# Block sums stored in one transfer each, and new places in the order for FFN weights, sum reads and three x tiles

## The chip, the cores and the metric

The kernel runs on one core of one Trainium2 chip. The metric is device time in microseconds (us), the median of several runs. A core has five engines that run side by side, each through its own instructions in order: TensorE (PE, matmuls; its weight loads are listed as PEld), VectorE (DVE), ScalarE (ACT), GpSimd (POOL) and SyncE (SP), which here issues all transfers to and from DRAM.

## The reference

One step of a hybrid layer over 128 context tokens and 1024 latent tokens of width 1024, in float32:

```
h  = rmsnorm(x) * (1 + scale1) + shift1
u  = h @ w_in                       # pool part, LRU part, gate part
mix = concat(pool_mixer(u_pool), rg_lru(conv(u_x)) * gelu(u_gate)) @ w_out
x  = x + gate1 * rmsnorm(mix)
h2 = rmsnorm(x) * (1 + scale2) + shift2
gu = h2 @ w_ffn_in                  # d_ff = 2816
x  = x + gate2 * rmsnorm((silu(gu[:d_ff]) * gu[d_ff:]) @ w_ffn_out)
```

The scales, shifts and gates come from a conditioning vector through a modulation matrix; the LRU is a gated linear scan in both directions.

## The kernel before, in words

The 1152 tokens are nine tiles of 128 rows (tile 0 is the context), in three groups of 384 columns once transposed. Each float32 operand is split into a rounded part and a rest (names with h or HT, and l or LO); a product is three matmuls, h*h, h*l and l*h. The helper `split` writes the rounded part by a copy (L315 on ACT, L317 on DVE, whichever the planner picks) and the rest by a subtraction on DVE (L346).

The code doesn't issue instructions directly. It lists operations, and a planner (class `Sched`) runs a model of the engines and takes again and again the operation that can start first; among equals the lower priority number wins, which is the place in the program plus `S.shift`. What it decides is each engine's order; on the chip each engine keeps to it and waits where something isn't there yet. Buffers come from small pools: three "raw" buffers of 512 KB, four "f", six "ring" and so on, and five banks "ps", two "pt", one "pm" for matmul results.

Stages that matter here:

- `stage_x(t)` loads an x tile, computes its root mean square (L309, L366 to L369), scales it (L456 or L458), transposes it by eight matmuls with the identity (L466, four to a bank) and copies the banks into stage buffers (L481, L483). `make_h` modulates these (L524, L526) and splits them into HT and LO. `gemm_in` (L533) multiplies them with w_in. Tiles 6 to 8 are the last column group; their gemm is 72 matmuls for the first three units of weights (`M0`).
- `mod_group` multiplies the second modulation matrix (L862: 16 matmuls in the order, 32 records in the trace).
- `post_mix(t)`, in the order of tiles 0, 4, 1, 5, 2, 6, 3, 7, 8, takes a tile's output gemm, multiplies it with the gate rows (L333, `s<-ps,grow`), norms it, adds it to x (L995), stores it (`x1d`), scales it (L456 or L458, `s<-xt,r`), transposes it (L466) and makes `hf`, HT and LO of the FFN.
- `combos(t)` for tiles 4 to 7 builds four sums of blocks of a pair of tiles, splits each into a raw buffer `tp` and stores it to the DRAM tensor `tdr` (L963).
- `FW(f)` loads one FFN weight block (two transfers of 512 KB, `rw<-in_w_fi`, into raw buffers) and `split` makes `wq` of it. `load_T` and `load_T1` read the sums back (`T`, and the right half of HT and LO). The FFN's first block is plain matmuls (L533 with `wq`), the later ones use the sums (L1235).

`combos` and `FW` share the raw pool; all transfers share SP's queue.

Of the kernel before, what the change touches and what calls it, by code (L numbers as in the profile page):

```python
# [7 lines left out]
F32 = mybir.dt.float32  # L8
# [34 lines left out]
TABLE_PEN = 400  # L43
DMA_AHEAD = 1.0
TABLE_WAIT = 1.0
TSH = (0, 60, 60)
STEPS = "p1 p8 p6 p2 tr8 p7 cx p5 xpz p4 p3 hi_gate hi_out store"
LASTK = 2
ORDER = "L0 F0 L1 F1 L2 P3 L3 P2 P1 P0 F2 F3"
# [2 lines left out]
KREV = (7,)  # L52
KG = 4
MODG = (1, 2, 2, 4)
LATE_STEP = 40
XPS = (1, 2)
SHIFTS = (-150, -100)
# [221 lines left out]
def kernel(ctx: ExitStack, tc: tile.TileContext, x, cT, vec, rows, w_modA, w_modB, w_in, w_gate,  # L279
                      w_pool, w_out, w_fi, w_fo, y, st_out):  # L280
    nc = tc.nc
# [3 lines left out]
    dram = ctx.enter_context(tc.tile_pool(name="dram", bufs=1, space=bass.MemoryType.DRAM))  # L285
# [3 lines left out]
    S = Sched(counts)  # L289

    def sb(name, tag="s", shape=(128, T), dt=F32, n=1):
        return S.buf(tag, lambda: sp.tile(list(shape), dt, name=name, tag=tag, bufs=counts[tag]), n)

    def bank(tag="ps"):
        return S.buf(tag, lambda: psp.tile([128, 512], F32, name=tag, tag=tag, bufs=counts[tag]))
# [39 lines left out]
    def dma(dst, src, w, r, nbytes, q="SP"):  # L335
        return S.op((("SP", nbytes / DMA_RATE),), lambda e: nc.sync.dma_start(dst(), src()), r, w)
# [7 lines left out]
    def split(src, h, l, w_h, w_l, r, n):  # L344
        anycopy(h, src, w_h, r, n)
        dve(lambda: nc.vector.tensor_tensor(l(), src(), h().bitcast(F32), op=OP.subtract), w_l, list(r) + list(w_h), n)  # L346

    class Unit:
        def __init__(self, src, tag="ring"):
            raw = sb("raw", "raw", (128, 1024))  # L350
            dma(lambda: raw.t, lambda: src, raw.all(), [], 524288)
            self.h = h = sb("uh", tag, (128, 1024), F32R)
            self.l = l = sb("ul", tag, (128, 1024), F32R)
            split(lambda: raw.t, lambda: h.t, lambda: l.t, h.all(), l.all(), raw.all(), 1024)
# [47 lines left out]
    def K(name, ks, ts):  # L402
        return (HT if name == "H" else LO).k(ks, ts)

    def TT(tg):
        return range(3 * tg, 3 * tg + 3)
# [65 lines left out]
    def stage_x(t):  # L472
        S.tag = f"x{t}"
        xt = xs.pop(t)

        def consume(g, pt):
            def fn(e):
                for i in range(4):
                    d, p = stage[4 * g + i].t[:, t * 128:(t + 1) * 128], pt.t[:, i * 128:(i + 1) * 128]
                    if e == "ACT":  # L480
                        nc.scalar.activation(d, p, AF.Copy)  # L481
                    else:
                        nc.vector.tensor_copy(d, p)  # L483
            S.op((("ACT", 0.65), ("DVE", 0.8)), fn, pt.all(), [stage[4 * g + i][t] for i in range(4)])
        norm_T(xt, consume, None, ("ps", "ps") if t in XPS else ("pt", "pt"))

    def mod_quarter(q, ws):
        S.tag = f"modq{q}"
        pm = bank("pt")
        g = MODG[q]  # L490
        for i in range(0, 4, g):
# [24 lines left out]
    def make_h(k, tg):  # L516
        S.tag = f"h{k}{tg}"
        parts = [(0, 128, 0), (128, 384, 1)] if tg == 0 else [(tg * TG, (tg + 1) * TG, 1)]
        sk = [stage[k][t] for t in TT(tg)]
        for a, b, v in parts:  # L520
            def mod(e, a=a, b=b, v=v):
                d, sc, bi = stage[k].t[:, a:b], s1[:, k, v:v + 1], b1[:, k, v:v + 1]
                if e == "ACT":
                    nc.scalar.activation(d, d, AF.Identity, bias=bi, scale=sc)  # L524
                else:
                    nc.vector.tensor_scalar(d, d, sc, bi, op0=OP.mult, op1=OP.add)  # L526
            S.op(c_act(b - a, ptr=2) + c_dve(b - a, True, 2), mod, [("mod1", k // 2)], sk)
        c = slice(tg * TG, (tg + 1) * TG)
        split(lambda: stage[k].t[:, c], lambda: HT[:, k, c], lambda: LO[:, k, c], K("H", [k], TT(tg)),
              K("L", [k], TT(tg)), sk, TG)  # L530
# [38 lines left out]
    def evac(m, tg, p):  # L569
        if m < 4:  # L570
            evac_x(m, tg, p)
        else:
            if m not in mix:
                mix[m] = sb(f"mix{m}", n=3)
            g = mix[m]
            anycopy(lambda: g.t[:, tg * TG:(tg + 1) * TG], lambda: p.t[:, :TG], [g[tg]], p.all(), TG, True)
# [4 lines left out]
    for a in START.split():  # L581
        i = int(a[1:])
# [30 lines left out]
    for m in M0:  # L613
        for tg in range(2):
            evac(m, tg, pend[m][tg])
    for t in range(6, 9):
        stage_x(t)
    for k in range(KT):
        make_h(k, 2)
    for m in M0:  # L620
        pend[m][2] = bank()
        gemm_in(wu[m], pend[m], range(KT), (2,))
        evac(m, 2, pend[m][2])
# [286 lines left out]
    for n, a in enumerate(ORDER.split()):  # L910
        j = int(a[1:])
# [34 lines left out]
    hfs = {}  # L946
    HN = 512
    PAIR = (4, 5, 6, 7)
    tdr = dram.tile([4, 4, 128, 2, HN], F32, name="tdr")

    def combos(t):

        S.tag = f"T{t}"
        a, b = hfs.pop(t - 4), hfs.pop(t)
        c = slice(t * 128, (t + 1) * 128)
        ca = slice((t - 4) * 128, (t - 3) * 128)
        b11, b21, b12, b22 = ((lambda h=h, i=i: h.t[:, 4 * i:4 * i + 4]) for h, i in ((a, 0), (a, 1), (b, 0), (b, 1)))
        k11, k21, k12, k22 = ([h[k] for k in range(4 * i, 4 * i + 4)] for h, i in ((a, 0), (a, 1), (b, 0), (b, 1)))
        def put(i, e):
            o = sb(f"tp{i}", "raw", (128, 2, 4, 128), F32R, n=2)  # L960
            split(lambda: e.t, lambda: o.t[:, 0], lambda: o.t[:, 1], [o[0]], [o[1]], e.all(), 512)
            for kt in range(4):
                S.op((("SP", 0.6),), lambda _, kt=kt: nc.sync.dma_start(  # L963
                    tdr[i - 1, kt, :, :, ca], o.t[:, :, kt].bitcast(F32)), o.all(), [("td", i, kt, t)])
        d = sb("d", "gw", (128, 4, 128))
        tt(lambda: d.t, b12, b11, d.all(), k12 + k11, 512, OP.subtract)
        put(1, d)
        e = sb("e", "gw", (128, 4, 128))
        tt(lambda: e.t, b22, b12, e.all(), k22 + k12, 512, OP.subtract)
        put(3, e)  # L970
        tt(lambda: e.t, lambda: e.t, b11, e.all(), k11, 512, OP.add)
        put(2, e)
        tt(lambda: e.t, b21, lambda: e.t, e.all(), k21, 512, OP.subtract)
        put(4, e)
# [46 lines left out]
    FORD = [f for i in range(HF) for f in (i, HF + i)]  # L1021

    class FW:

        def __init__(self, f):
            self.raw, self.q = [], []
            for i in range(2):
                raw = sb("rw", "raw", (128, 1024))  # L1030
                dma(lambda raw=raw, i=i: raw.t, lambda i=i: w_fi[f, i], raw.all(), [], 524288)
                self.raw.append(raw)

# [35 lines left out]
    for t in TORD:  # L1069
        if t not in pg:  # L1070
            gout(t)
        if t in TORD[:2]:
            continue
        for u in TORD[:3] if t == TORD[2] else (t,):
            post_mix(u, pg[u])
            if u in PAIR[:-1]:
                combos(u)
            if u == PAIR[-2]:
                fw0 = FW(FORD[0])
                fw0.split(0)  # L1080
                fw0.split(1)
    combos(PAIR[-1])
# [61 lines left out]
    def load_T(i):  # L1144
        S.tag = f"Tl{i}"
        for kt in range(4):
            o = TT_[i, kt] = sb(f"T{i}", "s", (128, 2, HN), F32R)
            dma(lambda o=o: o.t.bitcast(F32), lambda i=i, kt=kt: tdr[i - 1, kt], o.all(),
                [("td", i, kt, t) for t in PAIR], 524288)

    def load_T1():
        S.tag = "Tl1"
        c = slice(HN, 2 * HN)
        for kt in range(4):
            for j, (X, n) in enumerate(((HT, "H"), (LO, "L"))):
                dma(lambda kt=kt, X=X: X[:, kt, c].bitcast(F32), lambda kt=kt, j=j: tdr[0, kt, :, j], K(n, [kt], PAIR),
                    [("td", 1, kt, t) for t in PAIR], 262144)

    def operand(i, kt):
        if i in (1, "B11", "B21", "B22"):  # L1160
# [156 lines left out]
    load_T(2)  # L1317
    S.shift = TSH[0]
    load_T(3)
    S.shift = TSH[1]  # L1320
    load_T1()
    S.shift = TSH[2]
    load_T(4)
# [196 lines left out]
    p = product("E1", gsl(0, H1), gk(0), "11", t8)  # L1520
# [10 lines left out]
    p = product("E5", ssl(0), lambda kt: [("s12", kt)], "11", t8, ("11", "12", "11"))  # L1531
# [4 lines left out]
    p = product("E6", ssl(1), lambda kt: [("s12", kt)], "11", None, ("11", "22", "11"))  # L1536
# [4 lines left out]
    p = product("E7", gsl(0, H2), gk(0), "12", None, ("12", "22", "12"))  # L1541
# [4 lines left out]
    p = product("E4", gsl(HF, H2), gk(HF), "11", None, ("11", "11", "21"))  # L1546
# [7 lines left out]
    p = product("E2", gsl(HF, H1), gk(HF), "21", t8)  # L1554
# [8 lines left out]
    p = product("E3", ssl(2), lambda kt: [("s4", kt)], "22", t8, None, TAIL)  # L1563
# [3 lines left out]
    for n, (i, h) in enumerate(late):  # L1567
        S.shift = -LATE_STEP * n
        add(h[1], h[1], p[i])
# [89 lines left out]
```

## Time and profile before

| what | value |
|---|---|
| median of three runs | 1091.43 us (1089.12 to 1091.92) |
| profiled execution, its own time | 1093.47 us |
| its span in the trace | 1091.7 us |
| PE busy | 1070.3 us, 98% of the span |
| VectorE busy | 782.5 us, 72% |
| ScalarE busy | 491.2 us, 45% |
| the chain that ended last | 91% PE, 4% DVE, 2% DMA |

The span is the time from the first to the last recorded instruction of one execution; the run's own time lies 1.8 us above it. A busy share is a mean over stages: whether an engine ends a wait is read in the stage. The granted clock is PE's, 1.00 for 2.4 GHz and 0.50 for 1.2 GHz.

### The profile page before, as it was taken

What the parts mean: (1) busy time and instruction counts of PE and PEld (TensorE: products, weight loads), DVE (VectorE), ACT (ScalarE), POOL (GpSimd) and SP (SyncE); (2) the same over time, 40 slices, a digit from 0 to 9 for tenths busy, and PEclk for the clock granted to TensorE, in tenths of its full rate; (3) what the DMA queues carried; (4) which work ended last, traced back from release to release, by engine and by line L of the source; (5) the groups of instructions that cost most, each with busy time, mean ns of one, the idle gap of its engine ahead of it and who ended that gap; (6) DMA issues with size and microseconds to landing.
All of it is one profiled execution on the core that took longest, in us unless ns stands there. A gap on an engine that the chain in (4) does not pass through costs nothing.

```text
span 1091.7 us, 14516 instructions
## 1 busy us (share of the span) xinstructions
PE 1070.3 (98%) x5505; PEld 912.4 (84%) x5505; DVE 782.5 (72%) x1428; ACT 491.2 (45%) x891; POOL 8.8 (1%) x54
## 2 busy tenths in 40 slices
PE   7999999999999899999999999999999999999997
PEld 6988899998888888888888888888888888888885
DVE  5756899994987657658467575584667978878876
ACT  7656888872866423234233232332324223233331
POOL 0010000000000000000000000000000000000000
PEclk9989999999999899999999999999999999999999
DMA  9835631132555872314223233141246953353612
GB/s 364 314 120 210 217 117 44 59 133 99 181 186 155 283 287 82 111 39 150 82 68 113 86 102 111 39 150 73 78 154 223 379 174 105 88 175 107 217 53 97
DMA packets 68664, 158.88 MB, mean 146 GB/s; under 512 B 6241, under 2 KB 26097, under 8 KB 68593
## 3 DMA queue, kind: packets, MB, share of 16 engines
q1 hardware_dynamic: 68592, 157.95, 41.8%
q8 instruction: 43, 0.70, 0.3%
q14 instruction: 29, 0.23, 0.1%
HBM read 118.45 MB, written 39.47 MB: 145 GB/s over the span
## 4 chain that ended last, share of the span: by engine, by line
PE 91%; DVE 4%; DMA 2%; ACT 1%; issue 0%; SPq 0%; DVEq 0%; ACTq 0%
PE ps L533 33%; PE ps L1235 32%; PE pm L533 10%; PE pt L533 8%; PE pt L1235 5%; DMA raw<-in_w_in 2%; PE pm L862 1%; PE pt L466 1%; DVE e L333 1%; ACT jk L309 1%; DVE x L1496 1%; PE pt L496 1%; DMA rw<-in_w_fi 0%; DVE tp L346 0%; DVE s L333 0%
## 5 line engine op out<-in xcount | busy, mean ns | idle before, releaser
L533 PE MATMUL ps<-bw,au 128*128 128x512 f32 x627 | 164.4, 391 | 0.0
L533 PEld LDWEIGHTS ps<-bw,au 128*128 128x128 f32 x627 | 117.7, 188 | 25.8
L1235 PE MATMUL ps<-T,wu 128*128 128x512 f32 x504 | 123.1, 393 | 0.2
L1235 PE MATMUL ps<-HT,wu 128*128 128x512 f32 x336 | 111.4, 392 | 0.0
L1235 PEld LDWEIGHTS ps<-T,wu 128*128 128x128 f32 x504 | 92.8, 188 | 21.2 <-ACT wq L315 1.0
L315 ACT ACTIVATE au<-araw 128x512 fp32r<-128x512 f32 x73 | 46.0, 631 | 135.5 <-PE ps L533 88.6
L533 PE MATMUL ps<-HT,uh 128*128 128x384 f32 x280 | 84.9, 345 | 4.3 <-ACT HT L315 2.2
L533 PE MATMUL ps<-HT,ul 128*128 128x384 f32 x280 | 83.8, 341 | 1.3 <-DVE a L362 1.3
L533 PE MATMUL ps<-LO,uh 128*128 128x384 f32 x280 | 83.9, 341 | 0.1
L1235 PEld LDWEIGHTS ps<-HT,wu 128*128 128x128 f32 x336 | 63.1, 188 | 13.8
L1235 PE MATMUL ps<-LO,wu 128*128 128x512 f32 x168 | 65.5, 390 | 0.0
L309 ACT ACTIVATE g<-g 128x512 f32<-128x512 f32 x42 | 26.6, 632 | 83.7 <-DVE g L333 83.4
L315 ACT ACTIVATE wq<-rw 128x512 fp32r<-128x512 f32 x66 | 40.3, 628 | 52.7 <-DMA rw<-in_w_fi 46.2
L1235 PE MATMUL ps<-T,wq 128*128 128x512 f32 x252 | 61.0, 390 | 0.0
L533 PE MATMUL pm<-wq,HT 128*128 128x512 f32 x168 | 60.4, 397 | 0.0
L346 DVE TENSOR_TENSOR wq<-rw,wq 128x512 fp32r<-128x512 f32 x88 | 58.1, 684 | 2.9 <-ACT wq L315 2.7
L315 ACT ACTIVATE wu<-q 128x512 fp32r<-128x512 f32 x64 | 40.1, 632 | 42.1 <-DVE q L333 42.1
L333 DVE TENSOR_TENSOR wu<-q,wu 128x512 fp32r<-128x512 f32 x84 | 56.8, 686 | 1.8 <-ACT wu L315 1.4
L533 PEld LDWEIGHTS ps<-HT,uh 128*128 128x128 f32 x280 | 52.4, 192 | 6.6 <-issue 3.6
L1235 PE MATMUL ps<-HT,wq 128*128 128x512 f32 x168 | 56.6, 389 | 0.0
L1235 PE MATMUL pt<-HT,wq 128*128 128x512 f32 x168 | 55.7, 393 | 0.0
L533 PE MATMUL pt<-bw,au 128*128 128x512 f32 x198 | 55.1, 390 | 0.0
(314 smaller groups left out, 2211.5 us busy)
## 6 DMA issues: line engine op xcount, KB each, us to landing
rw<-in_w_fi SPq DMA_DIRECT2D x44, 512.0 KB
mraw<-in_w_modB SPq DMA_DIRECT2D x32, 512.0 KB
gdr<-g SPq DMA_DIRECT2D x21, 576.0 KB
araw<-gdr SPq DMA_DIRECT2D x20, 512.0 KB
xt<-in_x SPq DMA_DIRECT2D x18, 512.0 KB
wm<-in_w_modA SPq DMA_DIRECT2D x16, 512.0 KB
tdr<-tp SPq DMA_DIRECT2D x64, 128.0 KB
rows<-in_w_fo SPq DMA_DIRECT2D x16, 512.0 KB
```

The costliest lines, as they stand in the source:

```text
L309: nc.scalar.activation(dst(), src(), func, **k)
L315: nc.scalar.activation(dst(), src(), AF.Copy)
L333: return dve(lambda: nc.vector.tensor_tensor(dst(), a(), b(), op=op), w, r, n)
L346: dve(lambda: nc.vector.tensor_tensor(l(), src(), h().bitcast(F32), op=OP.subtract), w_l, list(r) + list(w_h), n)
L466: nc.tensor.transpose(pt.t[:, i * 128:(i + 1) * 128], xn.t[:, k * 128:(k + 1) * 128], ident)
L496: nc.tensor.matmul(pm.t[32 * j:32 * j + 32, 0:128], sT[:, kt].rearrange("p a b -> p (a b)"), ws[kt // 2].t[:, kt % 2, kind, kk * 128:(kk + ...
L533: nc.tensor.matmul(out, lhsT, rhs, start=first, stop=last)
L862: nc.tensor.matmul(pm.t[32 * j:32 * j + 32, 0:256], sT[:, kt].rearrange("p a b -> p (a b)"), raw.t[:, j * 256:(j + 1) * 256], start=kt == ...
L1235: nc.tensor.matmul(ps.t, w, m, start=first and kt == 0 and i == 0, stop=kt == 3 and i == 2, skip_group_check=not first)
L1496: dve(lambda c=c, a=a: nc.vector.scalar_tensor_tensor(x1.t[:, c], a(), r.t[:, 0:1], x1.t[:, c], op0=OP.mult, op1=OP.add), [x1[n]], r.all() ...
```

## The change

There are three parts, and all of them go through the planner.

1. `combos` stores a sum with one transfer of 512 KB in place of four of 128 KB (`tdr` gets another layout; each piece is 512 bytes as before). The planner counts 3.0 us for it (`TDT`) in place of 4 x 0.6. The reads of `load_T` take two runs of 2 KB per partition instead of one of 4 KB.
2. The operations of `stage_x` for tiles 6 to 8 get a priority 40 places earlier (`X6`); the reads of sums `load_T1` and `load_T(4)` get 100 places later instead of 60 (`TSH`).
3. The loads of the first FFN weights are listed before `post_mix(2)` instead of after tile 6's sums; their splits stay where they were.

```diff
-TSH = (0, 60, 60)
+TSH = (0, 100, 100)
+FWT = 2
+FWTAG = ("raw", "raw")
+TDT = 3.0
...
+X6 = -40
+H6 = 0
...
+    S.shift = X6
     for t in range(6, 9):
         stage_x(t)
+    S.shift = H6
     for k in range(KT):
         make_h(k, 2)
+    S.shift = 0
...
-    tdr = dram.tile([4, 4, 128, 2, HN], F32, name="tdr")
+    tdr = dram.tile([4, 128, 8, HN], F32, name="tdr")
...
-            for kt in range(4):
-                S.op((("SP", 0.6),), lambda _, kt=kt: nc.sync.dma_start(
-                    tdr[i - 1, kt, :, :, ca], o.t[:, :, kt].bitcast(F32)), o.all(), [("td", i, kt, t)])
+            S.op((("SP", TDT),), lambda _: nc.sync.dma_start(
+                tdr[i - 1, :, :, ca], o.t.rearrange("p a b n -> p (a b) n").bitcast(F32)), o.all(), [("td", i, t)])
...
+        if t == FWT:
+            fw0 = FW(FORD[0], FWTAG)
         for u in TORD[:3] if t == TORD[2] else (t,):
             post_mix(u, pg[u])
             if u in PAIR[:-1]:
                 combos(u)
             if u == PAIR[-2]:
-                fw0 = FW(FORD[0])
                 fw0.split(0)
                 fw0.split(1)
...
-            dma(lambda o=o: o.t.bitcast(F32), lambda i=i, kt=kt: tdr[i - 1, kt], o.all(),
-                [("td", i, kt, t) for t in PAIR], 524288)
+            dma(lambda o=o: o.t.bitcast(F32), lambda i=i, kt=kt: tdr[i - 1].rearrange(
+                "p (a b) n -> p a b n", a=2)[:, :, kt], o.all(), [("td", i, t) for t in PAIR], 524288)
...
-                dma(lambda kt=kt, X=X: X[:, kt, c].bitcast(F32), lambda kt=kt, j=j: tdr[0, kt, :, j], K(n, [kt], PAIR),
-                    [("td", 1, kt, t) for t in PAIR], 262144)
+                dma(lambda kt=kt, X=X: X[:, kt, c].bitcast(F32), lambda kt=kt, j=j: tdr[0, :, 4 * j + kt], K(n, [kt], PAIR),
+                    [("td", 1, t) for t in PAIR], 262144)
```

The new lines move the numbers of the code behind them: L466 becomes L471, L533 becomes L538, L336 becomes L341, L963 becomes L970, L346 becomes L351, L317 becomes L322.

What the planner makes of it shows at three places. The first is PE from about 52 us on: before, the last matmul on the second column group (`pm<-HT,ul`), then the transposes of x tiles 6 to 8 with a modulation group (L862) between them, then the first of the 72 matmuls.

```order
L533 MATMUL pm<-HT,ul 128x384
L466 MATMUL pt<-ident,xt 128x128 x8
L862 MATMUL pm<-mraw,sT 32x256 x16
L466 MATMUL pt<-ident,xt 128x128 x16
L533 MATMUL ps<-HT,uh 128x384
```

The same engine after the change, a piece from among the matmuls that stood ahead of the transposes before.

```order
L538 MATMUL ps<-HT,ul 128x384
L471 MATMUL pt<-ident,xt 128x128 x4
L538 MATMUL ps<-HT,uh 128x384
L538 MATMUL ps<-LO,uh 128x384
L538 MATMUL ps<-HT,ul 128x384
L471 MATMUL pt<-ident,xt 128x128 x4
```

The 24 transposes are now spread in groups of 8, 4, 4, 4 and 4 over 30 matmuls that ran ahead of them, and the modulation group stands behind the 72 matmuls.

The second place is SP's queue around the loads `rw` of the first FFN weights. Before, they stand behind the stores of tile 6's four sums (`tp_3455` to `tp_3523`), ahead of tile 7's first (`tp_3723`).

```order
L963 DMA tdr<-tp_3471 256x1x128 x4
L336 DMA x1d<-xt 128x1024
L963 DMA tdr<-tp_3499 256x1x128 x4
L963 DMA tdr<-tp_3523 256x1x128 x4
L336 DMA rw<-in_w_fi 128x1024 x2
L336 DMA x1d<-xt 128x1024
L963 DMA tdr<-tp_3723 256x1x128 x3
```

After, the same queue from tile 5's last two sums to tile 6's first two.

```order
L970 DMA tdr<-tp_3265 1024x1x128
L970 DMA tdr<-tp_3310 1024x1x128
L341 DMA rw<-in_w_fi 128x1024 x2
L341 DMA x1d<-xt 128x1024
L341 DMA xt<-in_x 128x1024
L970 DMA tdr<-tp_3435 1024x1x128
L970 DMA tdr<-tp_3462 1024x1x128
```

The loads moved ahead of tile 6's four stores, a store of x and a load of an x tile, and each sum is one row instead of four.

The third place is VectorE around the splits of these weights (`wq`). Before, they stand together, between the scaling of tile 7 and the first product of tile 8 with the gate row.

```order
L458 TENSOR_SCALAR s<-xt,r 128x1024
L346 TENSOR_TENSOR wq<-rw,wq 128x512 x2
L317 CAST wq<-rw 128x512
L346 TENSOR_TENSOR wq<-rw,wq 128x512 x2
L1009 TENSOR_SCALAR hf<-pt,s_76,b_77 128x128 x4
L333 TENSOR_TENSOR s<-ps,grow 128x512
```

After, the first pair of them stands among tile 6's sums.

```order
L351 TENSOR_TENSOR tp_3435<-d,tp_3435 128x512
L338 TENSOR_TENSOR e<-hf 128x512
L351 TENSOR_TENSOR wq<-rw,wq 128x512 x2
L338 TENSOR_TENSOR ss<-ss_3386 128x1
L367 TENSOR_SCALAR a<-ss 128x1
L351 TENSOR_TENSOR tp_3462<-e,tp_3462 128x512
```

And the second pair stands ahead of tile 7's residual sum (`xt<-s,r,xt`), after which tile 7's scaling and then tile 8's products follow with no split between them.

```order
L322 CAST wq<-rw 128x512
L351 TENSOR_TENSOR wq<-rw,wq 128x512 x2
L1002 SCALAR_TENSOR_TENSOR xt<-s,r,xt 128x1024
L322 CAST HT<-hf 128x4x128
L351 TENSOR_TENSOR LO<-hf,HT 128x4x128 x2
L367 TENSOR_SCALAR a<-ss 128x1
```

The same four subtractions and one copy now lie some 30 rows apart and earlier.

## Rows read from the trace of the kernel before

**Rows 1.** The page: busy time of engines; shares of the chain that ended last.
```profile
PE 1070.3 (98%) x5505; PEld 912.4 (84%) x5505; DVE 782.5 (72%) x1428; ACT 491.2 (45%) x891; POOL 8.8 (1%) x54
...
PE 91%; DVE 4%; DMA 2%; ACT 1%; issue 0%; SPq 0%; DVEq 0%; ACTq 0%
```

**Rows 2.** Waits of PE: us in total, times, longest.
```profile
PE pt L466 <- ACT s L456: 3.7, 1, 3.7
...
PE ps L533 <- DVE HT L317: 1.7, 1, 1.7
...
PE pt L466 <- ACT st L481: 0.7, 2, 0.4
```

**Rows 3.** Windows: length, busy by engine, granted clock, DMA share, GB/s.
```profile
62.00:64.00 2.00, 1.43 (x11) 0.84 (x9) 0.97 (x5) 1.25 (x8) 0.00 (x0) 1.00 0.99 401
64.00:66.00 2.00, 0.41 (x1) 0.29 (x1) 2.00 (x8) 2.00 (x5) 0.00 (x0) 0.83 1.01 401
66.00:68.00 2.00, 2.00 (x6) 1.75 (x6) 2.00 (x6) 2.00 (x5) 0.00 (x0) 0.50 0.83 272
...
360.00:362.00 2.00, 1.81 (x9) 1.81 (x10) 0.28 (x1) 0.79 (x3) 0.00 (x0) 0.50 0.89 248
```

**Rows 4.** The chain that ended last, 52 to 82 us: start, us, what.
```profile
52.23 5.20 PE ps L533 x30
...
59.35 1.86 PE pm L862 x32
...
65.59 15.93 PE ps L533 x72
```

**Rows 5.** Timeline, 49 to 66 us: start, us, engine, what [idle before <- releaser].
```profile
49.84 0.75 DVE L458 TENSOR_SCALAR xt<-xt,r 128x1024 f32<-128x1024 f32 x1
...
58.31 1.04 PE L466 MATMUL pt<-ident,xt 128*128 128x128 f32 x8
...
58.99 0.17 DVE L650 TENSOR_SCALAR sm<-sm 128x8 f32<-128x8 f32 x1 [6.28 <-POOL sm L646]
...
65.64 1.96 DVE L346 TENSOR_TENSOR LO<-st,HT 128x384 fp32r<-128x384 f32 x4
```

**Rows 6.** The chain that ended last, 339 to 375 us.
```profile
339.27 4.97 DMA rw<-in_w_fi
...
360.19 1.97 PE pt L466 x8
362.16 12.09 PE ps L533 x60
```

**Rows 7.** Timeline, 344 to 361 us, ACT, DVE and PE.
```profile
344.27 1.16 ACT L315 ACTIVATE wq<-rw 128x512 fp32r<-128x512 f32 x2 [3.44 <-DMA rw<-in_w_fi]
...
344.93 1.29 DVE L346 TENSOR_TENSOR wq<-rw,wq 128x512 fp32r<-128x512 f32 x2 [2.67 <-ACT wq L315]
...
345.65 0.39 PE L533 MATMUL pm<-uh,LO 128*128 128x512 f32 x1
...
349.03 0.68 DVE L333 TENSOR_TENSOR s<-ps,grow 128x512 f32<-128x512 f32 x1
...
355.96 0.51 PE L533 MATMUL ps<-HT,wq 128*128 128x384 f32 x2
...
358.99 1.15 ACT L456 ACTIVATE s<-xt,r 128x1024 f32<-128x1024 f32 x1 [0.83 <-DVE r L369]
```

**Rows 8.** Window of 139 to 255 us.
```profile
139.00:255.00 116.00, 116.00 (x671) 112.05 (x670) 114.02 (x132) 92.89 (x120) 1.40 (x13) 1.00 0.29 97
```

**Rows 9.** Tiles tdr and a on SP: ns min/median/max, first to last start.
```profile
L963 SPq DMA_DIRECT2D tdr<-tp x64: 512/618/1591, 288.9 to 367.6; - x64
...
L336 SPq DMA_DIRECT2D a<-gdr x4: 319/368/3529, 804.4 to 869.9; - x4
```

**Rows 10.** Timeline of SP, tile 5's fourth sum.
```profile
315.91 2.59 SPq L963 DMA_DIRECT2D tdr<-tp  x4
```

More of the change, by code (lines that the diff above doesn't have):

```diff
@@ L1023, with __init__ @@
     class FW:
-        def __init__(self, f):
+        def __init__(self, f, tags=("raw", "raw")):
             self.raw, self.q = [], []
             for i in range(2):
-                raw = sb("rw", "raw", (128, 1024))
+                raw = sb("rw", tags[i], (128, 1024))
                 dma(lambda raw=raw, i=i: raw.t, lambda i=i: w_fi[f, i], raw.all(), [], 524288)
```

## The prediction

> **What bounds the kernel now.** I read the page first. TensorE (PE) is busy 98% of the span and the chain that ended last is 91% PE [rows 1]. So time can come only from PE idle time, or from stretches in which PE is busy at the lower of its two clocks. Second, the chain of waits for PE [rows 2]: the longest, 3.7 us, is a transpose (L466) that waits for ScalarE's scaling of a tile (L456); two others, 1.7 us for HT (L317) and 0.7 us for stage copies (L481), belong to one place. Third, windows of 2 us around these [rows 3]: after each wait the granted clock falls from 1.00 to 0.50 (2.4 to 1.2 GHz), so a wait is paid twice. There are two such places, and the change touches both. Elsewhere in what is moved PE has no wait to win back.
>
> **Place 1, x tiles 6 to 8 (52 to 82 us).** Before, 36 matmuls run first, 30 of them in 5.20 us, so 0.1733 each [rows 4]; only then come the 24 transposes of x tiles 6 to 8, eight in 1.04 us at full clock [rows 5], in lockstep with the copies that empty their banks. Behind them PE waits for HT, and 72 matmuls then take 15.93 us [rows 4] instead of 72 x 0.1733 = 12.48, since the clock is at 0.50 in their first part [rows 3]. Work at full clock from 52.23 to the end at 65.59 + 15.93 = 81.52: 36 x 0.1733 + 24 x 0.13 + 1.86 (the modulation group L862) + 12.48 = 6.24 + 3.12 + 1.86 + 12.48 = 23.70. The stretch lasts 29.29, so 5.6 us are lost: 2.1 idle and 3.45 of clock.
> After, the transposes stand among the 36 matmuls in groups of 8 and 4, so copies have other PE work to hide behind. Their inputs are there in time: the last of the three tiles is scaled at 49.84 + 0.75 [rows 5], before 52.23. The modulation group moves behind the 72 matmuls; its cost moves and doesn't change. New cost: VectorE makes a LO piece in 1.96/4 = 0.49 us [rows 5], about what the first 24 of the 72 matmuls eat it at (3 x 0.1733 = 0.52), with casts between, and it starts late if it stands behind L650, which waits for GpSimd until 58.99 [rows 5]. Bounds: 0 (the pace holds) and 2.1 (the whole old wait). I take 0.7, nearer the first, because only part of eight pieces is exposed. **Place 1: -5.6 + 0.7 = -4.9.**
> The work behind it starts earlier with PE. Its tightest stretch is 139 to 255 us, where VectorE is busy 114.02 of 116 us [rows 8]; PE is busy all of it. VectorE's own work there starts from PE's results, so it should move with them. If it didn't, up to all 4.9 would be lost there: this is in the rivals.
>
> A rule speaks against the interleaving: the Trainium skill, "TensorE: Matmul & The Clock Gate", Part 4, says of transposes that they don't count as PE-busy in the same way as matmuls and don't engage the full clock. The window 62 to 64 stands at 1.00 with 16 transposes around it [rows 3], and eight transposes at 58.31 take 1.04 us against 1.97 at half clock at 360.19 [rows 5, 6]; so the trace doesn't agree that they run at the low clock. By the rule 3.45 us of clock would stay lost here and the sum would be 1085; it is the fourth rival.
>
> **Place 2, first FFN weights (336 to 374 us).** Before, the two loads of rw are issued at 339.27 behind tile 6's stores and land 4.97 us later [rows 6]. ScalarE and VectorE reach the splits of rw before it is there: their in-order queues stand 3.44 and 2.67 us [rows 7]. Behind those splits stands tile 8's norm: its product with the gate row (s<-ps) starts at 349.03, though its gemm's matmuls have been issued by 345.65. Its scaling starts at 358.99 and takes 1.15, and PE, whose last matmul ahead starts at 355.96, waits 3.72 for it [rows 2, 7]. Then the clock is 0.50 [rows 3]: eight transposes take 1.97 instead of 1.04 (0.93) and 60 matmuls 12.09 instead of 60 x 0.1733 = 10.40 (1.69) [rows 6]. In all 3.72 + 0.93 + 1.69 = 6.3 us.
> After, the loads stand behind tile 5's four stores, issued at about 315.91 + 2.59 = 318.5 [rows 10], and land near 323.5, before their splits are due. Nobody waits for rw. Tile 8's product can start at about 346.0, when its gemm ends, 3.0 us sooner; its scaling then ends at 358.99 + 1.15 - 3.0 = 357.1. PE has 6 more matmuls ahead of the transposes (the 6 that stood behind tile 8's in the old order): it comes at 355.96 + 2 x 0.17 + 6 x 0.1733 = 357.3. So the wait goes, with no slack to speak of.
> What is late next: two of the three "raw" buffers hold rw while tile 6's sums run, so these go through fewer buffers, and 3.0 us of split work (at 344.93 it ran in VectorE's idle time) now stand between tile 6's and tile 7's instructions. Bounds of this: 0, and 3.0 (all of it lands on tile 8's chain). I take 1.5: half, since tile 6's sums are also late work that nobody on PE waits for soon. **Place 2: -6.3 + 1.5 = -4.8.**
>
> **One store per sum.** 48 of 64 stores go. Four of them took 4 x 0.62 us of SP's issue time, spaced about 0.65 (2.59 for a sum) [rows 9, 10]. The nearest rows for a transfer in about a thousand pieces are the reads a<-gdr, 0.37 us as median and 3.53 at most [rows 9]. So an issue goes from 2.6 to between 0.4 and 3.5 us a sum: -2.2 to +0.9, off PE's chain, where SP is not waited for except through rw. I take 0 at both ends; in the worst case 16 x 0.9 spread over 80 us is hidden by SP's idle time. The T reads come in 2 KB pieces rather than 4 KB, the same bytes; they and the second rw load keep their distance to PE's need (the second load stands behind tile 7's stores as before). Cost 0 while a load is less than about 4 us late; beyond that it is the slower rival.
>
> **Sum.** -4.9 - 4.8 = -9.7. The profiled execution took 1093.47: 1083.8. The median of the runs, 1091.43, is 2.04 below that execution, so a median of about 1081.7, said as 1082. Own range of this case: 1078.5 (both places give all, -11.9, and a little of run-to-run difference) to 1085 (both new costs at their upper bounds, -4.9 + 1.4 - 4.8 + 1.5 = -6.8).
>
> **Rivals.** *One place gives nothing* (chance 0.20): tile 8 stays late because splits and sums now compete for buffers, 1091.43 - 4.9 = 1086.5; or VectorE's full stretch swallows place 1, 1091.43 - 4.8 = 1086.6. For it: no slack at 357, VectorE at 98% from 139 to 255. Against: no PE wait in that stretch today.
> *No change* (0.11): the new order brings two new PE waits elsewhere, each with its clock: 2.1 + 3.45 = 5.6 and 3.7 + 2.6 = 6.3 are what such a wait costs in this trace, and two of them give 1091 back. For it: the order of all engines from 52 to 420 us is new. Against: today such waits number two in that length.
> *Slower* (0.08): a merged store keeps its raw buffer until 512 KB have landed. If a store took 3.53 to issue and 4.97 to land as rw does, 8.5 us, tile 7's four through few buffers would end about 17 us later than today; the second load of rw stands behind them, and PE would idle about 12 us and then run some 3 us slower: 1081.7 + 15 = 1097. It decides where a store takes more than about 7.5 us, so that 13 us are lost.
> *Transposes hold the clock down* (0.07), as a mechanism of place 1: its 72 matmuls take 15.93 again; 1081.7 + 3.45 = 1085.
>
> **How the numbers follow.** The forecast itself has 0.54. What a measurement of this kernel can tell is about 0.3%, 3.3 us: faster means below 1088.2. Forecast, one place and transposes lie below: 0.54 + 0.20 + 0.07 = 0.81; same 0.11; slower 0.08. The range runs from 1078.5 over the one-place cases to 1089, which leaves out the slower case and most of no change.
>
> **What would show it.** Right: no PE wait for HT L317's successor or for the scaling of tile 8 above 1 us; granted clock 1.00 in all windows from 52 to 80 and from 345 to 370; the 72 matmuls in about 12.5 to 13.2 us; rw issued near 312 to 319 and its splits without idle time ahead of them; the first L1235 matmul some 10 us earlier than before. Wrong: a wait of over 2 us for a tile's scaling, for tp buffers or for T, with a window at 0.50 behind it; or the shift of place 1 present at 82 us and gone by 255.

## The result, and the profile after

The changed kernel takes 1084.86 us (median of 4 runs, 1084.62 to 1085.48) against 1090.81 us for the kernel before (1089.12 to 1091.92): a ratio of 0.9948, 95% interval 0.9930 to 0.9965, so 5.9 us or 0.5% faster. The forecast of 1082 lies 2.9 us below; its range of 1078.5 to 1089 holds the time. The profiled execution took 1084.80 us, its span is 1083.0 us, 8.7 us less than the span before. So the two traces differ by 8.7 us and the medians by 5.9; that gap is one of the questions below. Two runs at a lower granted clock, 1182.07 us of the last kernel below and 2095.60 us of the kernel before, are left out of all figures.

The page of the changed kernel, busy time of engines and shares of the last chain, beside [rows 1]:

```profile
PE 1063.7 (98%) x5505; PEld 907.0 (84%) x5505; DVE 781.2 (72%) x1425; ACT 486.7 (45%) x890; POOL 9.6 (1%) x54
...
PE 91%; DVE 3%; DMA 3%; ACT 1%; POOL 0%; issue 0%; SPq 0%; DVEq 0%; ACTq 0%
```

Its waits of PE, beside [rows 2]:

```profile
PE ps L538 <- DVE LO L351: 1.9, 2, 1.7
...
PE pt L471 <- ACT st L486: 0.8, 2, 0.4
...
PE ps L1243 <- ACT v L320: 0.7, 1, 0.7
...
PE pt L471 <- ACT s L461: 0.4, 1, 0.4
```

The 3.7 us for tile 8's scaling are gone (what is left at that line, 0.4, is tile 3's). The wait for HT at place 1 has a successor of nearly the same length in this execution: 1.7 us for a LO piece. Windows of 2 us at the two places, beside [rows 3] (length, busy time of PE, PEld, DVE, ACT and POOL, granted clock, DMA share, GB/s):

```profile
62.00:64.00 2.00, 0.30 (x3) 0.29 (x3) 2.00 (x8) 1.95 (x5) 0.00 (x0) 1.00 0.00 0
64.00:66.00 2.00, 2.00 (x13) 2.00 (x13) 2.00 (x6) 1.61 (x3) 0.00 (x0) 1.00 0.00 0
...
354.00:356.00 2.00, 2.00 (x17) 1.97 (x16) 1.90 (x5) 1.99 (x4) 0.00 (x0) 1.00 1.04 289
```

PE stands still for 1.7 us from 62 to 64 and the clock stays at 1.00 behind it; at 354 us there is neither a wait nor a low clock. The chain that ended last shows what the stretches cost now, beside [rows 4, 6]:

```profile
63.71 12.61 PE ps L538 x71
...
354.74 0.87 PE pt L471 x8
355.62 9.37 PE ps L538 x54
```

The matmuls of place 1 run at full speed (12.61 / 71 = 0.178 us each, where 15.93 / 72 = 0.221 was), and so do those behind tile 8's transposes (9.37 / 54 = 0.174). Who holds PE at 62 us shows in the timeline: VectorE stood idle for 3.32 us until GpSimd ended its chain at 60.7, since a small instruction (L658) that waits for it stands in its queue ahead of the splits.

```profile
60.78 0.17 DVE L658 TENSOR_SCALAR sm<-sm 128x8 f32<-128x8 f32 x1 [3.32 <-POOL sm L654]
...
63.71 0.44 PE L538 MATMUL ps<-LO,uh 128*128 128x384 f32 x1 [1.70 <-DVE LO L351]
```

Last, the stores of the sums on SP, beside [rows 9] (ns, least, median, most, then first and last start):

```profile
L970 SPq DMA_DIRECT2D tdr<-tp x16: 512/516/627, 285.5 to 355.2; - x16
```

A store in 1024 pieces takes SP 0.52 us, near the lower of the two bounds (0.4 and 3.5), instead of 4 x 0.62.

Of the signs that the prediction named, most came: the clock at both places, the 71 recorded matmuls in 12.61 us, rw issued early (311.16 us) and its splits without a wait, the first of the FFN's L1243 matmuls at 369.0 us instead of 378.3. One didn't: the wait above 1 us at place 1.

### The profile page after: what moved, and what is told of

It reads as the page before. It is cut to its first block, busy times and chain, and to the rows that moved or that the text cites. A ratio compares the mean times of both kernels' runs of the same rounds, so it can differ in the third digit from the quotient of the medians.

```text
span 1083.0 us, 14446 instructions
## 1 busy us (share of the span) xinstructions
PE 1063.7 (98%) x5505; PEld 907.0 (84%) x5505; DVE 781.2 (72%) x1425; ACT 486.7 (45%) x890; POOL 9.6 (1%) x54
## 4 chain that ended last, share of the span: by engine, by line
PE 91%; DVE 3%; DMA 3%; ACT 1%; POOL 0%; issue 0%; SPq 0%; DVEq 0%; ACTq 0%
PE ps L538 33%; PE ps L1243 32%; PE pm L538 10%; PE pt L538 8%; PE pt L1243 5%; DMA raw<-in_w_in 2%; PE pm L870 1%; DMA xt<-in_x 1%; PE pt L471 1%; DVE x L1504 1%; DVE e L338 1%; ACT jk L314 0%; DVE LO L351 0%; PE pt L501 0%; DVE s L338 0%
## 5 line engine op out<-in xcount | busy, mean ns | idle before, releaser
L538 PE MATMUL ps<-bw,au 128*128 128x512 f32 x627 | 164.5, 391 | 0.0
L538 PEld LDWEIGHTS ps<-bw,au 128*128 128x128 f32 x627 | 117.7, 188 | 25.7
L1243 PE MATMUL ps<-T,wu 128*128 128x512 f32 x504 | 123.1, 393 | 0.7 <-ACT v L320 0.7
L1243 PE MATMUL ps<-HT,wu 128*128 128x512 f32 x336 | 112.0, 392 | 0.0
L1243 PEld LDWEIGHTS ps<-T,wu 128*128 128x128 f32 x504 | 92.7, 188 | 21.6 <-ACT v L320 1.1
L538 PE MATMUL ps<-HT,uh 128*128 128x384 f32 x280 | 84.5, 343 | 3.0 <-ACT HT L320 2.2
L538 PE MATMUL ps<-LO,uh 128*128 128x384 f32 x280 | 82.9, 337 | 1.9 <-DVE LO L351 1.9
L538 PE MATMUL ps<-HT,ul 128*128 128x384 f32 x280 | 82.9, 337 | 1.3 <-DVE ul L351 1.3
L1243 PEld LDWEIGHTS ps<-HT,wu 128*128 128x128 f32 x336 | 63.1, 188 | 13.8
L1243 PE MATMUL ps<-LO,wu 128*128 128x512 f32 x168 | 65.5, 390 | 0.0
L1243 PE MATMUL ps<-T,wq 128*128 128x512 f32 x252 | 61.3, 390 | 0.0
L538 PE MATMUL pm<-wq,HT 128*128 128x512 f32 x168 | 60.4, 397 | 0.0
L351 DVE TENSOR_TENSOR wq<-rw,wq 128x512 fp32r<-128x512 f32 x88 | 58.2, 685 | 0.3
L1243 PE MATMUL ps<-HT,wq 128*128 128x512 f32 x168 | 57.1, 389 | 0.0
L538 PEld LDWEIGHTS ps<-HT,uh 128*128 128x128 f32 x280 | 51.5, 189 | 6.4 <-issue 2.5
L1243 PE MATMUL pt<-HT,wq 128*128 128x512 f32 x168 | 55.7, 393 | 0.0
L538 PE MATMUL pt<-bw,au 128*128 128x512 f32 x198 | 55.1, 390 | 0.0
```

Of the source, the lines that this page charges most:

```text
L538: nc.tensor.matmul(out, lhsT, rhs, start=first, stop=last)
L1243: nc.tensor.matmul(ps.t, w, m, start=first and kt == 0 and i == 0, stop=kt == 3 and i == 2, skip_group_check=not first)
```

## The experiments

Times are medians; "before" is the kernel before in the same set of runs, 1090.4 to 1090.7 us.

**The parts alone, on the kernel before.** First, the kernel before itself, unchanged, for a second profile.

> The kernel before, unchanged. Its profiled execution took 1093.47 us, 2.7 above the median of its runs. First theory: how long TensorE stays at half clock behind its two waits (66 us and 360 us) differs from execution to execution, so a second profile has a time nearer 1090.8 and loses 1 to 4 us less in the 72 matmuls behind the first wait or in the 60 behind the second, with the same waits. Rival: the excess is spread over the span, and the 72 matmuls take 15.9 us and the 60 take 12.1 us again. The ratio should hold 1.000 within 0.2%.

1090.96 us (11 runs, 1088.74 to 1093.09), ratio 1.000 (0.9991 to 1.0009). Its profiled execution took 1093.09 and shows both clock falls in full again. From its last chain:

```profile
65.50 15.95 PE ps L533 x72
...
360.01 1.97 PE pt L466 x8
361.97 12.15 PE ps L533 x60
```

Here the rival came true: the two traced executions are alike, and both belong to the longest of the kernel's runs. The 29 runs of the kernel before beside it, without a trace, went from 1088.36 to 1092.91.

Second, x tiles 6 to 8 earlier, alone.

```diff
+    S.shift = -40
     for t in range(6, 9):
         stage_x(t)
+    S.shift = 0
```

> The kernel before with the earlier priority of x tiles 6 to 8 alone. First theory: place 1 gains by itself; with the new wait of 1.7 us that the changed kernel shows at 62 us, the stretch up to the end of the 72 matmuls is 3.3 us shorter in the trace, and the time falls by 1.5 to 3.3 us (less where the kernel before loses less clock in its usual runs). Rival: VectorE's full stretch from 139 to 255 us or the late FFN weights swallow it, and the time stays within 0.7 us of before.

1089.14 us (12 runs, 1085.91 to 1093.37), ratio 0.9990 (0.9978 to 1.0002). The median falls by 1.6 us, within what was expected, but the interval holds no change. Its trace surprises at place 2. Windows and timeline there:

```profile
354.00:356.00 2.00, 0.00 (x0) 0.00 (x0) 1.90 (x8) 1.14 (x4) 0.00 (x0) 1.00 0.91 325
356.00:358.00 2.00, 1.51 (x12) 1.52 (x13) 0.96 (x3) 1.25 (x4) 0.00 (x0) 1.00 0.94 266
```

```profile
356.49 1.09 PE L466 MATMUL pt<-ident,s 128*128 128x128 f32 x8 [3.35 <-ACT s L456]
```

PE waits 3.35 us for tile 8, as before, and the clock doesn't fall: the eight transposes take 1.09 us, not 1.97.

Third, the first FFN weights earlier, alone.

```diff
+        if t == 2:
+            fw0 = FW(FORD[0])
         for u in TORD[:3] if t == TORD[2] else (t,):
...
             if u == PAIR[-2]:
-                fw0 = FW(FORD[0])
```

> The kernel before with the first FFN weights loaded two tiles earlier, alone, the sums in four stores each as before. First theory: the wait of 3.7 us at 356 us and the half clock behind it go, about 6 us in the trace, and the time falls by 3.5 to 6 us. Rival: with two of three raw buffers taken by the weights, the sums of tile 6 need the merged store to pass through what is left; then TensorE waits for tile 7 or 8 again by over 2 us and less than 2 us are gained.

1092.55 us (11 runs, 1088.09 to 1093.92), ratio 1.0016 (1.0005 to 1.0026): slower, if by little. The rival was right in its mechanism and too low in its price, and the tile was another, 3. PE's transposes of tile 3 and ScalarE's queue in its timeline:

```profile
340.04 1.97 PE L466 MATMUL pt<-ident,s 128*128 128x128 f32 x8 [4.61 <-ACT s L456]
```

```profile
323.12 0.63 ACT L315 ACTIVATE wq<-rw 128x512 fp32r<-128x512 f32 x1 [6.05 <-DMA rw<-in_w_fi]
...
334.65 0.63 ACT L315 ACTIVATE tp<-e 128x512 fp32r<-128x512 f32 x1 [3.75 <-DMA tdr<-tp]
```

The wait moved from tile 8 to tile 3, the next in the order behind tile 6, and grew to 4.6 us, with the low clock behind it. ScalarE waits 6.05 us for the weights and then 3.75 us for a raw buffer: with the weights in two of three, a sum's buffer comes free only when its four stores have landed. At place 1, where nothing was changed, this execution has the same wait for HT as before, and the clock doesn't fall:

```profile
66.24 0.41 PE L533 MATMUL ps<-HT,uh 128*128 128x384 f32 x1 [1.73 <-DVE HT L317]
```

```profile
66.00:68.00 2.00, 1.52 (x7) 1.29 (x8) 2.00 (x6) 2.00 (x5) 0.00 (x0) 1.00 0.99 365
```

Fourth, one store per sum, alone.

```diff
-            for kt in range(4):
-                S.op((("SP", 0.6),), lambda _, kt=kt: nc.sync.dma_start(
+            S.op((("SP", 3.0),), lambda _: nc.sync.dma_start(
+                tdr[i - 1, :, :, ca], o.t.rearrange("p a b n -> p (a b) n").bitcast(F32)), o.all(), [("td", i, t)])
```

> The kernel before with one store of 512 KB per sum and the reads that go with it, alone. First theory: SP's issue time isn't waited for, the time stays within 0.8 us of before. Rival: shorter queueing ahead of the first FFN weights brings these up to 2 us earlier and wins 1 to 3 us at 356 us; or stores that land later hold their buffers longer and lose 1 to 3 us.

1086.93 us (5 runs, 1086.03 to 1088.44), ratio 0.9965 (0.9953 to 0.9978): 3.8 us faster, the largest effect of any part. My theory of no effect fell; the rival's direction held and its size, 1 to 3 us, was a little too small. Its SP queue and PE's transposes of tile 8:

```profile
326.38 7.54 SPq L962 DMA_DIRECT2D tdr<-tp  x4
334.00 1.73 SPq L336 DMA_DIRECT2D rw<-in_w_fi  x2
```

```profile
355.60 1.03 PE L466 MATMUL pt<-ident,s 128*128 128x128 f32 x8
```

The weights are issued at 334.00, not 339.27 [rows 6], although nothing asked for them earlier, and tile 8's transposes wait for nobody. So this part alone mends place 2. At place 1 it keeps the wait of 1.73 us for HT, and the clock is low behind it until about 71 us:

```profile
68.00:70.00 2.00, 2.00 (x8) 2.00 (x8) 2.00 (x7) 1.81 (x4) 0.00 (x0) 0.50 0.14 41
```

**Parts taken back, on the changed kernel.** GpSimd's chain, which the planner takes for 5.0 us, counted at 7.0:

```diff
-    pool(lsig2, [("ls",)], [("e",), ("z",), ("zz",)], 5.0)
+    pool(lsig2, [("ls",)], [("e",), ("z",), ("zz",)], 7.0)
```

> The changed kernel, with the planner's cost of GpSimd's small chain at 7.0 us instead of 5.0 (it takes 6.2 in the trace); in the order this moves only two small VectorE instructions behind the 18 pieces of copies and splits that stood behind them. First theory: VectorE's idle time of 3.3 us until 60.8 us, and with it TensorE's wait of 1.7 us for a LO piece, comes from these two waiting for GpSimd; the wait falls below 0.5 us and the time falls by 1.2 to 2 us against the changed kernel, to 1083.2 or below. Rival: the pieces of the last column group are late anyway, from the transposes and the copies, and the wait stays above 1 us.

1083.69 us (5 runs, 1083.41 to 1085.10), ratio 0.9941 (0.9928 to 0.9953). In its trace VectorE comes to L658 without idle time, and PE has no wait for LO left:

```profile
66.66 0.17 DVE L658 TENSOR_SCALAR sm<-sm 128x8 f32<-128x8 f32 x1
```

The median is 1.2 us lower than the changed kernel's 1084.86, at the lower end of what was expected and not quite at 1083.2; four of its five runs lie below all runs of the changed kernel. The first theory holds for the wait; that the wait is what the 1.2 us are isn't shown, since it differs from trace to trace (see the run with the reads at their old priority, below).

Without the earlier x tiles:

```diff
-X6 = -40
+X6 = 0
```

> The changed kernel without the earlier priority of x tiles 6 to 8. First theory: the two waits of place 1 and the half clock are back, and the time lies 1.5 to 3.3 us above the changed kernel, 1086.4 to 1088.2. Rival: place 1 gives nothing in usual runs, and the time is 1084.9 within 0.7.

1086.22 us (5 runs, 1085.72 to 1087.81), ratio 0.9963 (0.9951 to 0.9975): 1.4 us above the changed kernel, just below what the first theory had. Its trace has the old wait at place 1:

```profile
64.00:66.00 2.00, 0.41 (x1) 0.19 (x1) 2.00 (x8) 2.00 (x5) 0.00 (x0) 1.00 1.02 414
66.00:68.00 2.00, 1.83 (x10) 1.83 (x11) 2.00 (x6) 2.00 (x5) 0.00 (x0) 1.00 0.78 264
```

```profile
65.52 0.41 PE L538 MATMUL ps<-HT,uh 128*128 128x384 f32 x1 [1.73 <-DVE HT L322]
```

PE waits 1.73 us for HT, as in [rows 2], and the clock stays at 1.00. So in this execution the 3.45 us of clock of [rows 3, 4] weren't there to be won, and what the earlier x tiles changed was one wait of 1.7 us for another.

With four stores (the layout and the reads go back too):

```diff
-            S.op((("SP", TDT),), lambda _: nc.sync.dma_start(
-                tdr[i - 1, :, :, ca], o.t.rearrange("p a b n -> p (a b) n").bitcast(F32)), o.all(), [("td", i, t)])
+            for kt in range(4):
+                S.op((("SP", 0.6),), lambda _, kt=kt: nc.sync.dma_start(
+                    tdr[i - 1, kt, :, :, ca], o.t[:, :, kt].bitcast(F32)), o.all(), [("td", i, kt, t)])
```

> The changed kernel with four stores per sum and the old layout of the sums. First theory: the merged store is worth nothing, 1084.9 within 0.8. Rival: the merged store is what lets tile 6's sums through one or two raw buffers; then TensorE waits over 1 us for a tile's scaling near 335 or 355 us and the time is 1 to 4 us above the changed kernel.

1090.75 us (12 runs, 1085.15 to 1092.57), ratio 0.9992 (0.9978 to 1.0005): all of the gain is gone. The rival held, at more than the size it gave. The profiled execution was one of the short ones, 1085.86. A second profile of it:

> The changed kernel with four stores per sum once more, for a second profile: its runs went from 1085.2 to 1092.6 while the profiled one took 1085.9. First theory: in a longer execution the same instructions wait longer for transfers between 300 and 370 us (stores of sums or the weights behind them), so that tile 7's or 8's scaling is late by 2 us or more than in the first profile, and the clock falls to 0.50 behind it. Rival: the waits are the same to 0.5 us, and only the clock behind them differs. If the time is within 1 us of 1085.9 it tells nothing.

It took 1089.78 us. The order is the same; PE's transposes of tile 3 in the first and then in the second:

```profile
336.08 1.09 PE L471 MATMUL pt<-ident,s 128*128 128x128 f32 x8 [2.27 <-ACT s L461]
```

```profile
338.81 1.97 PE L471 MATMUL pt<-ident,s 128*128 128x128 f32 x8 [5.11 <-ACT s L461]
```

And ScalarE's waits for transfers ahead of it, first and second:

```profile
320.05 0.63 ACT L320 ACTIVATE wq<-rw 128x512 fp32r<-128x512 f32 x1 [4.56 <-DMA rw<-in_w_fi]
...
330.06 0.63 ACT L320 ACTIVATE tp<-e 128x512 fp32r<-128x512 f32 x1 [2.23 <-DMA tdr<-tp]
```

```profile
322.42 0.63 ACT L320 ACTIVATE wq<-rw 128x512 fp32r<-128x512 f32 x1 [7.04 <-DMA rw<-in_w_fi]
...
333.43 0.63 ACT L320 ACTIVATE tp<-e 128x512 fp32r<-128x512 f32 x1 [3.23 <-DMA tdr<-tp]
```

ScalarE waits 2.5 and 1.0 us longer for the weights and a buffer in the longer execution, PE's wait grows by 2.8 us, and the low clock follows. The first theory holds, for tile 3: the weights are issued 0.8 us later (315.85 against 315.04) and take 1.6 us more until ScalarE can use them, so how long transfers take differs from execution to execution, and this kernel has them on PE's chain.

With the sum reads at their old priority:

```diff
-TSH = (0, 100, 100)
+TSH = (0, 60, 60)
```

> The changed kernel with the reads of the sums at their old priority. First theory: the new place of the reads behind the next weights is worth nothing or at most the wait of 0.7 us that the changed kernel has at L1243; 1084.9 within 0.8. Rival: the weights that stood behind the reads come late again and TensorE waits over 1 us near 370 to 390 us, 1086 or above.

1084.94 us (5 runs, 1084.72 to 1084.97): no difference from 1084.86. That part is worth nothing. Its trace has the same order at place 1 as the changed kernel, but a much shorter wait for LO:

```profile
62.67 0.45 PE L538 MATMUL ps<-LO,uh 128*128 128x384 f32 x1 [0.33 <-DVE LO L351]
```

Over the six traces with the earlier x tiles and the chain at 5.0 this wait is 0.30, 0.33, 0.33, 0.70, 0.95 and 1.70 us; the longest is that of the changed kernel's profile.

With the weights in their old place:

```diff
-FWT = 2
+FWT = -1
...
             if u == PAIR[-2]:
+                fw0 = FW(FORD[0], FWTAG)
```

> The changed kernel with the first FFN weights loaded behind tile 6's sums again, as before. The merged store alone took the wait of 3.7 us at 356 us away and the earlier weights alone made a wait of 4.6 us for tile 7. First theory, which took the place of my own: the merged store is what mends place 2, and the earlier weights add nothing; 1084.9 within 0.8, with no wait over 1 us for a tile's scaling. Rival, that of the prediction: the earlier weights are needed, the splits stand in front of tile 8 again, and the time is 1086.5 or above.

1084.78 us (5 runs, 1083.28 to 1085.21), ratio 0.9942 (0.9928 to 0.9956). The first theory holds: the earlier weights add nothing once the store is one.

**What the single store gains by.** One store, with SP's issue time given back by tiny transfers:

```diff
+            def store():
+                nc.sync.dma_start(tdr[i - 1, :, :, ca], o.t.rearrange("p a b n -> p (a b) n").bitcast(F32))
+                for j in range(3):
+                    nc.sync.dma_start(tdx[i - 1, t - 4, j], o.t[0:8, 0, j].bitcast(F32))
+            S.op((("SP", 3.0),), lambda _: store(), o.all(), [("td", i, t)])
```

> The kernel before with one store per sum, and behind each of these three tiny transfers (8 pieces of 512 bytes to a scratch tensor) that give SP back the issue time of four, in the same order of all engines. With one store the first FFN weights were issued at 334.0 us instead of 339.3 and the wait for tile 8 was gone. First theory: it is SP's issue time of about 0.6 us per transfer, eight stores in a row, that made the weights late; with the tiny transfers they are issued 3 to 5 us later than with one store alone, the wait of over 2 us for tile 8's scaling is back, and the time is 1089 or above. Rival: the time lies with the transfers themselves (four small ones land later than a large one); then the time stays at 1086.9 within 1, though SP issues as much as before.

1087.79 us (9 runs, 1085.79 to 1088.32), ratio 0.9972 (0.9963 to 0.9982): 2.6 us below the kernel before, and 0.9 above one store alone, which the two intervals (0.9953 to 0.9978 there) don't tell from nothing. Its SP queue:

```profile
334.08 0.52 SPq L965 DMA_DIRECT2D tdr<-tp  x1
334.64 1.98 SPq L967 DMA_DIRECT2D tdx<-tp  x3
336.67 0.83 SPq L336 DMA_DIRECT2D rw<-in_w_fi  x2
```

The weights are issued 2.7 us later than with one store alone, a little less than the 3 to 5 expected, and tile 8's wait doesn't come back. The first theory fell, and the time lies within the rival's 1 us of 1086.9. But the run gives back only half of what it was to give back: the kernel before issues the weights at 339.27, another 2.6 us later. So SP's issue time isn't ruled out as a cause; what is shown is that half of it costs little, 0.9 us in medians.

Another part is the order. By counting 3.0 us for a store where it counted 4 x 0.6, the planner also puts a store of x behind the loads of the weights, ScalarE's squares of tile 8 (`jk<-ps`) ahead of its product with the gate row, and a split of tile 7's sums behind tile 8's own work. In VectorE's rows of the kernel before, tile 8's residual sum stands at 355.37 behind a tp split at 354.76; with one store alone it stands at 350.58, and both tp splits come after it:

```profile
350.58 1.28 DVE L994 SCALAR_TENSOR_TENSOR xt<-s,r,xt 128x1024 f32<-128x1024 f32 x1
351.77 0.68 DVE L346 TENSOR_TENSOR tp<-d,tp 128x512 fp32r<-128x512 f32 x1
```

What the order is worth can be read from the instruction behind the last split of the weights (`hf`) to the end of tile 8's scaling. The kernel before, whose scaling is in [rows 7], and then the one with tiny transfers:

```profile
347.75 1.36 DVE L1009 TENSOR_SCALAR hf<-pt,s,b 128x128 f32<-128x128 f32 x4
```

```profile
345.06 1.37 DVE L1013 TENSOR_SCALAR hf<-pt,s,b 128x128 f32<-128x128 f32 x4
...
354.53 0.75 DVE L458 TENSOR_SCALAR s<-xt,r 128x1024 f32<-128x1024 f32 x1
```

That is 12.4 us before (347.75 to 358.99 + 1.15) and 10.2 with the new order (345.06 to 354.53 + 0.75). So the scaling ends 4.9 us earlier, 2.7 by weights that are split earlier and 2.2 by the order behind them; by these rows neither alone would take away all of the 3.72 us. How the 2.7 divide between SP's queue and the transfers themselves, and what four transfers in this order would take in runs, stays open.

**The two best together.** The weights' old place and the chain at 7.0 us:

> The changed kernel with the weights' old place (1084.8 in its own runs) and GpSimd's chain at 7.0 us in the planner (1083.7 on the changed kernel): the two versions that tied or beat it, together. First theory: the wait of 1.7 us goes here too, though that kernel's profile shows only 0.3 us of it; 1083.0 to 1084.5. Rival: there was nothing of that wait left to win with the old place, and it stays at 1084.8 within 0.4.

1083.21 us (5 runs, 1083.08 to 1084.57), ratio 0.9936 (0.9924 to 0.9949), in the range of the first theory. It beats both kernels, by about 1.6 us the changed one, and ties with the chain at 7.0 us alone. Only 0.30 us of the wait for LO were there to go in the trace of the kernel that it is compared with (the weights' old place), so what the rest of the gain is isn't shown.

## Why the prediction was right and wrong

**Sign and range: right.** Faster was forecast with 0.81, and the time lies in the range. The two places were the right ones to look at: the waits and low clocks that left the trace are those two, and 300 to 372 us now has 71.6 us of PE work where it had 68.3. That the sum came so near is in part luck: place 2's gain came from the part that was priced at nothing, and place 1 gave less than a third of its sum in runs.

**"I take 0 at both ends" for the merged store: wrong, and the main failure.** The step said that SP isn't waited for except through rw, and put that at nothing. Yet the prediction had itself put the loads of rw behind tile 6's stores: the exception was place 2. One store alone gives -3.8 us; four stores on the changed kernel lose 5.9. The issue time was sized well (0.52 us in bounds of 0.4 to 3.5). What the step left out is what hangs on the store: the weights behind it (issued at 334.00 instead of 339.27) and the order that the planner makes of a cost of 3.0, worth 2.2 us on tile 8's chain.

**Place 2, -4.8 for the earlier weights: the gain is there, its cause isn't.** Earlier weights alone are 1.8 us slower in medians, and they add nothing to one store (1084.78 without, 1084.86 with). The step that failed is the one that bounded the cost of tile 6's sums going through fewer raw buffers to 0 to 3.0 us, by VectorE's split work; the cost is a wait for stores to land, 3.75 us on ScalarE, and it fell on tile 3, which the step didn't follow. With one store per sum PE's wait for tile 3 is down to 0.39 us.

**Place 1, -4.9: right mechanism, wrong size.** The order took the transposes out of lockstep and the 71 matmuls run at full clock. Between the two traces the same work ends 3.3 us sooner (78.19 us with the modulation group against 81.52); in runs the order is worth 1.4 us on the changed kernel. Two terms were off. The new cost, taken as 0.7, is 1.70 for LO and 0.35 for a transpose in the changed kernel's profile: 2.05, about its upper bound, because L658 stands ahead of the splits as the step feared. Since the wait for LO is 0.30 to 0.95 us in the other five traces of this order, 0.7 was low for that execution more than for the kernel. And the 3.45 us of clock were counted as lost in every execution. The traces show the same wait of 1.7 us with the clock low until 72 us (before, twice), until about 71 us (one store alone) and 70 us (with tiny transfers), and not low at all (earlier weights alone, and the changed kernel without the earlier x tiles).

**"2.04 below that execution, so a median of about 1081.7": wrong.** The excess of the profiled execution of before over its median was carried over to the changed kernel, whose profiled execution is at its median (1084.80 and 1084.86). The trace's own difference, 8.7 us, is within 1.0 of the sum of -9.7; the medians differ by 5.9. Both traced executions of before (1093.47 and 1093.09) have both clock falls in full, 3.45 + 2.6 us, and other executions of the same waits have shorter ones or none. The mean granted clock, which is on record for every run, bears this out in part. The two traced executions stand at 0.991 and 0.990. Of the 80 runs of the kernel before among the experiments, the four at 0.990 took 1092.12 to 1093.09 us and the three at 0.996 took 1089.22 to 1089.63, but the 24 at 0.994 took anything from 1088.36 to 1092.52. So the clock is one part of the spread, and what the other is wasn't traced for this kernel.

**Rivals.** That transposes hold the clock down is out: it stands at 1.00 through all windows with transposes among the matmuls. That its time, 1085, is nearest to the measured one is chance. The merged store landing late is out: from 300 to 372 us no wait of ScalarE or VectorE in the changed kernel ends with a store. "One place gives nothing" (1086.5 or 1086.6) is nearer in kind, since place 1 gave 1.4 of its 4.9 us in runs, but not by the ways it named: tile 8 isn't late, and from 139 to 255 us PE is busy all of the time in the changed kernel too, with VectorE at 108.4 of 116 us.

**Size by part**, in runs: one store 3.8 (on the kernel before), earlier x tiles 1.4, earlier weights 0, reads 0 (on the changed kernel). The sum, 5.2, is near the 5.9 of the whole. The parts aren't independent: on the changed kernel, whose earlier weights share the raw buffers, the store is worth 5.9.

## What to carry to other kernels

A row that costs nothing on its own engine can still be what a critical transfer queues behind: price an edit to a queue by what stands behind it and, where a planner makes the order, by the order that its new cost makes; price a load that takes buffers from a small pool by the landing time of the stores that free the rest. Where the kernel's runs spread by some us and one profile is at hand, look where that profile stands in the spread before using its losses as gains; a clock fall behind a wait is a chance, not a fixed price. A duration in a planner that is too short (5.0 for a chain of 6.2 us) puts a waiting instruction ahead of work that was ready: correcting it lowered the median by 1.2 us.

## What the runs showed of the hardware

The same PE wait had different sequels. After 1.7 us at place 1 the clock was at 0.50 until 72 us in the two traces of before, until about 71 and 70 us in two others, and stayed at 1.00 with the earlier weights alone and without the earlier x tiles. After 3.5 to 3.7 us for tile 8 it fell, and after 3.35 us for the same tile with earlier x tiles it didn't.

The same program's transfers took different times. The first FFN weights of one kernel, issued at 315.04 and 315.85 us in two executions, were there for ScalarE 5.0 and 6.6 us later.

The spread of run times goes with the kernel, but not with the number of stores alone. Its standard deviation is 1.0 us for the kernel before (69 runs beside the others) and for one store alone (5 runs), 0.9 with tiny transfers (9 runs), 1.7 to 2.4 us for the three other kernels with four stores per sum (11 or 12 runs each), and 0.1 to 0.9 for the changed kernel and the others with one store (4 or 5 runs each).
